# The opening of a decoder trunk: the first norm's modulation as one TensorE product in four column groups, squares on two engines, and an order written by hand

## The chip, the cores and the metric

The kernel runs on one core of a Trainium2 chip. A core has a matrix engine (TensorE, PE in the profile, with its weight loads shown apart as PEld), three engines for elementwise work (VectorE or DVE, ScalarE or ACT, GpSimd or POOL) and a queue engine (SyncE or SP) that issues most of the DMAs. The engines run side by side and wait for each other by semaphores. The metric is the device time of one execution in microseconds.

## The reference, cut to what matters

The program is a trunk of two layers over 512 tokens of width 1024, each of them an FFN half step, a mixing block and a second FFN half step. Each sub-layer begins with a norm that is modulated by the conditioning vector c:

```
c_act = silu(c)                                        # (1, 1024)
mod   = (c_act @ w_ada[l] + b_ada[l])                  # 9 rows of 1024: shift, scale, gate, ...
hn    = x * rsqrt(mean(x * x) + eps) * g * (1 + scale) + shift
h     = h + 0.5 * (1 + gate) * swiglu(hn, w_ffn1_in, w_ffn1_out)
```

Only the first norm of the first layer is touched here. It needs x, c, and the columns of `w_ada[0]` for the first shift and the first scale: 1024 by 2048 numbers in f32, 8 MB. Nothing can be multiplied before this norm has its first rows, so it is the opening of the program.

## The kernel before

Activations lie transposed: `h[0]` to `h[7]` are eight tiles of 128 channels by 512 tokens, loaded as `in_xT`. A normed activation is kept as a pair, `hnH` (rounded to the matrix engine's format fp32r) and `hnL` (the rest), and so are weights (`wH`, `wL`, made by `split` from a loaded f32 tile: a copy on ScalarE, L93, then a subtraction on VectorE, L94). `mm3` multiplies such pairs with three matmuls: wH by hnH (L88), wH by hnL (L89) and wL by hnH (L90).

`begin` (from L1064) is the opening. It loads c, an identity, the eight tiles of x and the parameters, then by `fetch(m)` the modulation's weights `wa0`, in four steps m of 2 MB, each for two tiles of channels, and between them by `fetch_w` the first four weight tiles of the FFN. All of these DMAs are issued on SP's queue in the order of the code, two for each `fetch`.

- c is spread over the 128 partitions by eight matmuls against the identity and a silu (`crep`, L1120 to L1125).
- The squares of the tiles of x are taken by ScalarE (`add_ss`, L191 and L198) and added one by one by VectorE into one tile (`ss`, L194). Four f32 matmuls against a column of ones (L1142) make sums over the channels; an f32 matmul is two instructions, so the profile has eight. ScalarE takes the square root (its table is loaded just before, L1145), VectorE the reciprocal (L1146), and four matmuls spread the result over the partitions (`ps_rstd`, L1149).
- `warm(n)` puts n matmuls on ones in front of PE, whose results nobody reads.
- `scales(m)` makes the two scale columns of step m on VectorE: each is a dot of a 128 by 1024 tile with `crep` (`ada_dot`, L151), then a small operation (L1092). `shifts(m)` makes one shift column in the same way and the other by eight f32 matmuls of one column (16 instructions, L1100).
- `normed(k)` applies the norm to tile k: times rstd on VectorE (L1105), scale and shift on ScalarE (L1107), then `split`.
- Then four output tiles of the FFN's first projection are built up over the eight channel tiles: 4 steps m, in each 8 `mm3`, which are 96 matmuls in all. In step m, after the second `mm3`, the scales, shifts and normed tiles for step m + 1 are written.

The framework's scheduler may reorder all of this on each engine by priority; the code's order is not binding. Behind the opening, `ffn` goes on with the next weight tiles through two buffers, and spends VectorE's time also on the other modulation rows (`ada_steps`, through `wadaT`, issued on GpSimd's queue); their buffers lie in memory that the opening's pool gives back.

Of the kernel before, what the change touches and what calls it, by code (L numbers as in the profile page):

```python
# [16 lines left out]
P = 128  # L17
D = 1024
T = 512
L = 2  # L20
KD = D // P
# [4 lines left out]
NB = T // P  # L26
# [31 lines left out]
def trunk_kernel(ctx, tc, ins, out, layers=L, phases=("ffn1", "mix", "ffn2")):  # L58
    nc = tc.nc
# [18 lines left out]
    def psum(shape, name, tag="x"):  # L78
        return ps.tile(shape, F32, name=name, tag=tag, bufs=2)
# [5 lines left out]
    def mm3(acc, w, k, x, sl, start, stop):  # L85

        wH, wL, xH, xL = w[0][:, k], w[1][:, k], x[0][:, sl], x[1][:, sl]
        mm(acc, wH, xH, start=start, stop=False)  # L88
        mm(acc, wH, xL, start=False, stop=False)  # L89
        mm(acc, wL, xH, start=False, stop=stop)  # L90

    def split(hi, lo, src):
        nc.scalar.copy(hi, src)  # L93
        nc.vector.tensor_sub(lo, src, hi.bitcast(F32))  # L94

    ALL = slice(0, T)
# [4 lines left out]
    cT = const.tile([P, KD], F32, name="cT")  # L101
# [3 lines left out]
    h = []  # L105
    for i in range(KD):
        t = hp_.tile([P, T], F32, name=f"h{i}")
# [5 lines left out]
    cact = const.tile([P, KD], F32, name="cact")  # L113
# [35 lines left out]
    def ada_dot(out_, w, crep):  # L149

        stt(w, w, 1.0, crep, ALU.mult, ALU.mult, accum_out=out_)  # L151
# [31 lines left out]
    def new_ss():  # L183
        return sp.tile([P, T], F32, name="ss", tag="ss")

    def add_ss(ss, i, sl=ALL):

        if ss is None:
            return
        if i == 0:  # L190
            act(ss[:, sl], h[0][:, sl], AF.Square)  # L191
        else:
            sq = square(i, sl)
            tt(ss[:, sl], ss[:, sl], sq, ALU.add)  # L194

    def square(i, sl):
        sq = E("sq")[:, sl]
        act(sq, h[i][:, sl], AF.Square)  # L198
        return sq
# [863 lines left out]
    def begin(pool):  # L1063
        hn = [tuple(hnp.tile([P, T], F32R, name=n, tag="hn") for n in ("hnH", "hnL")) for _ in range(KD)]  # L1064
        g1 = prm(0, "g1")
        bsh, bsc = (prm(0, "b_ada")[:, i * KD : (i + 1) * KD] for i in range(2))
        col = {n: pool.tile([P, KD], F32, name=n, tag=n) for n in ("sc", "sh", "gb", "gm0", "sh0")}
        stt(col["gb"], bsc, 1.0, g1, ALU.add, ALU.mult)
        wa, wf, ws = {}, [], []

        def fetch(m):
            for n in (0, 2):
                w = pool.tile([P, 2, D], F32, name="wada", tag="wada", bufs=8)
                nc.sync.dma_start(w, ins["wa0"][m, :, n : n + 2])
                wa[m, n], wa[m, n + 1] = w[:, 0], w[:, 1]
# [12 lines left out]
        def scales(m):  # L1088
            for n in range(2):
                k = slice(2 * m + n, 2 * m + n + 1)  # L1090
                ada_dot(col["sc"][:, k], wa[m, n], crep)
                stt(col["gm0"][:, k], col["sc"][:, k], g1[:, k], col["gb"][:, k], ALU.mult, ALU.add)  # L1092

        def shifts(m):
            k0, k1 = (slice(2 * m + n, 2 * m + n + 1) for n in range(2))
            ada_dot(col["sh"][:, k0], wa[m, 2], crep)
            tt(col["sh0"][:, k0], col["sh"][:, k0], bsh[:, k0], ALU.add)
            pt = psum([P, 1], "ps_ada")
            for k in range(KD):
                mm(pt, wa[m, 3][:, k * P : (k + 1) * P], cact[:, k : k + 1], start=k == 0, stop=k == KD - 1)  # L1100
            tt(col["sh0"][:, k1], pt, bsh[:, k1], ALU.add)

        def normed(k):
            z = E("z")
            tt(z, h[k], rstd, ALU.mult)  # L1105
            x = E("hn_t")
            act(x, z, AF.Identity, bias=col["sh0"][:, k : k + 1], scale=col["gm0"][:, k : k + 1])  # L1107
# [10 lines left out]
        warm(3)  # L1118

        crep = pool.tile([P, D], F32, name="crep", tag="crep")  # L1120
        for hf in range(2):
            pt = psum([P, 4, P], "ps_crep")
            for k in range(4):
                mm(pt[:, k], cT[:, 4 * hf + k : 4 * hf + k + 1].to_broadcast([P, P]), cst("ident"), start=True, stop=True)
            act(crep[:, hf * 512 : hf * 512 + 512], pt.rearrange("p k n -> p (k n)"), AF.Silu)  # L1125
        fetch(0)
        fetch_w()
        fetch_w()
        fetch(1)
        fetch_w()  # L1130
        fetch_w()
        fetch(2)
        fetch(3)
        nc.sync.dma_start(con[:, P:], ins["con"][:, P:])
        warm(20)
        ss = new_ss()
        for i in range(KD):
            add_ss(ss, i)

        pt = psum([P, NB], "ps_ss")  # L1140
        for b in range(NB):
            mm(pt[:, b : b + 1], ss[:, b * P : (b + 1) * P], ones[:, :1], start=True, stop=True)  # L1142
        warm(3)
        r = pool.tile([P, NB], F32, name="rstd_t", tag="rstd_t")
        act(r, pt, AF.Sqrt, bias=vals["eps"], scale=1.0 / D)  # L1145
        nc.vector.reciprocal(r, r)  # L1146
        rstd = psum([P, T], "ps_rstd", "r0")
        for b in range(NB):
            mm(rstd[:, b * P : (b + 1) * P], r[:, b : b + 1].to_broadcast([P, P]), cst("ident"), start=True, stop=True)  # L1149
        warm(2)  # L1150
        scales(0)
        shifts(0)
        warm(8)
        normed(0)
        split_w(0)
        split_w(1)
        normed(1)
        pts = [psum([P, T], "ps_mm", tag) for tag in ("mm", "mm", "r1", "r0")]
        for m in range(4):
            groups = [(n, 2 * m + k) for k in range(2) for n in range(4)]  # L1160
            if m == 0:
                groups = [(n, k) for n0 in (0, 2) for k in range(2) for n in (n0, n0 + 1)]
            elif m == 3:
                groups = [(n, 6 + k) for n in range(4) for k in range(2)]
            for g, (n, k) in enumerate(groups):
                mm3(pts[n], ws[n], k, hn[k], ALL, k == 0, k == KD - 1)
                if m < 3 and g == 1:
                    scales(m + 1)
                    shifts(m + 1)
                    if m == 0:  # L1170
                        split_w(2)
                        split_w(3)
                    normed(2 * m + 2)
                    normed(2 * m + 3)
# [29 lines left out]
def lay_out(i):  # L1204
    import numpy as np

    a = {}
    c = np.ascontiguousarray
# [3 lines left out]

    wT = i["w_ada"].reshape(L, D, 9, KD, P).transpose(0, 2, 3, 4, 1)
    a["wadaT"] = c(wT)
    last = i["w_ada"][0, :, :D].reshape(KD, P, 4, 2, P)[:, :, :, 1].transpose(2, 1, 0, 3).reshape(4, P, D)
    a["wa0"] = c(np.stack([wT[0, 1, ::2], wT[0, 1, 1::2], wT[0, 0, ::2], last], axis=2))
# [41 lines left out]
    r, s = np.arange(P)[:, None], np.arange(P)[None, :]  # L1258
# [26 lines left out]
```

## Time and profile before

| | us |
|---|---|
| median of 3 runs | 1956.05 (1954.79 to 1958.45) |
| span of the profiled execution | 1949.5 |
| PE busy | 1899.8 |
| VectorE busy | 1402.5 |
| ScalarE busy | 839.5 |

The profile gives the span of one execution, from its first instruction to the end of its last. The runs' times are measured apart from it, on the device, and the median lies 6.6 us above the span. In a line of the timeline stand the start, the duration, the engine, the line of the code, the operation with the tiles it writes and reads, the shapes, and a count when several are merged; in brackets stands the idle time of the engine before it and what ended it. In a line of the groups stand, behind the count, the busy time, the mean duration of one in ns, and the idle time before them. A row of the windows view has a stretch, its length, then for PE, PEld, DVE, ACT and POOL the busy time and the number of instructions, then the clock granted to PE (1.00 is full), the share of the DMA engines, and GB/s. The matmuls overlap in PE's pipeline, so the step from one start to the next tells more than the duration of one.

### The profile page before, as it was taken

To read this page: it belongs to the slowest core of one execution; us is meant where nothing else is said; L and a number is where in the kernel's file an instruction comes from. 1 tells how busy PE (TensorE), PEld (TensorE's weight loads), DVE (VectorE), ACT (ScalarE), POOL (GpSimd) and SP (SyncE) were. 2 spreads that over 40 slices of the span, in tenths; PEclk is the share of its full clock that TensorE was granted. 3 is DMA by queue.
4 is the path that set the end of the run, shared out by engine and by line. 5 is a ranking of instruction groups with operands and counts; after the bars stand their busy time and mean duration, and the time that the engine had idled before them with its cause. 6 is when DMAs were issued, how large, how long until landed. Compare 5 with 4: busy or idle time off the path is not lost.

```text
span 1949.5 us, 33127 instructions
## 1 busy us (share of the span) xinstructions
PE 1899.8 (97%) x13544; PEld 1666.5 (85%) x13544; DVE 1402.5 (72%) x2176; ACT 839.5 (43%) x1269; POOL 131.2 (7%) x212
## 2 busy tenths in 40 slices
PE   8999999999999999999999999999998999999999
PEld 6898899885677899899899989988766788998997
DVE  7687677757975787677868767776488778773862
ACT  4453255346332454155345514533553335532541
POOL 0101101100000000100100021010000000010000
PEclk8999999999999999999999999999999999999999
DMA  7667865611121475875646587662211125764732
GB/s 294 245 166 236 251 193 163 219 67 38 49 81 51 141 195 172 285 207 168 228 129 189 161 273 220 175 214 102 87 53 49 59 72 158 197 210 136 194 107 91
DMA packets 104311, 308.21 MB, mean 158 GB/s; under 512 B 23392, under 2 KB 24416, under 8 KB 103136
## 3 DMA queue, kind: packets, MB, share of 16 engines
q1 hardware_dynamic: 75936, 203.34, 30.5%
q0 software_dynamic: 28224, 102.77, 20.5%
q8 instruction: 106, 1.74, 0.4%
q14 instruction: 45, 0.37, 0.1%
HBM read 302.66 MB, written 3.41 MB: 157 GB/s over the span
## 4 chain that ended last, share of the span: by engine, by line
PE 70%; DVE 11%; DMA 10%; issue 4%; ACT 3%; POOL 1%; SPq 0%; ACTq 0%; POOLq 0%; DVEq 0%
PE ps_mm L88 11%; PE ps_mm L89 10%; PE ps_mm L90 10%; PE ps_d L369 6%; PE ps_d L371 6%; PE ps_d L370 6%; PE ps_f L369 3%; PE ps_f L371 3%; PE ps_f L370 3%; DMA wada<-in_wadaT 3%; DVE wL L94 2%; ACT wH L93 2%; PE ps_g L371 2%; PE ps_g L370 2%; PE ps_g L369 2%
## 5 line engine op out<-in xcount | busy, mean ns | idle before, releaser
L93 ACT CAST wH<-wraw 128x1024 fp32r<-128x1024 f32 (+2 forms) x292 | 269.7, 924 | 534.5 <-PE ps_mm L89 250.6
L94 DVE TENSOR_TENSOR wL<-wraw,wH 128x1024 fp32r<-128x1024 f32 (+2 forms) x292 | 309.2, 1061 | 128.7 <-ACT wH L93 127.5
L88 PE MATMUL ps_mm<-hnH,wH 128*128 128x512 f32 (+1 forms) x760 | 277.6, 371 | 9.7 <-DVE lo L552 3.4
L88 PE MATMUL ps_mm<-actH,wH 128*128 128x512 f32 (+1 forms) x744 | 282.0, 379 | 0.0
L89 PE MATMUL ps_mm<-actL,wH 128*128 128x512 f32 (+1 forms) x744 | 282.0, 379 | 0.0
L90 PE MATMUL ps_mm<-actH,wL 128*128 128x512 f32 (+1 forms) x744 | 281.7, 379 | 0.0
L89 PE MATMUL ps_mm<-hnL,wH 128*128 128x512 f32 (+1 forms) x760 | 274.8, 363 | 0.4
L90 PE MATMUL ps_mm<-hnH,wL 128*128 128x512 f32 (+1 forms) x760 | 273.4, 361 | 0.5 <-DVE wL L94 0.5
L369 PE MATMUL ps_d<-comH,wH 128*128 128x256 f32 x816 | 227.8, 279 | 3.9 <-ACT s L391 3.8
L370 PE MATMUL ps_d<-comL,wH 128*128 128x256 f32 x816 | 225.9, 277 | 0.0
L371 PE MATMUL ps_d<-comH,wL 128*128 128x256 f32 x816 | 225.6, 276 | 0.0
L151 DVE SCALAR_TENSOR_TENSOR wada<-wada,crep 128x1024 f32<-128x1024 f32 x140 | 168.0, 1221 | 53.2 <-DMA wada<-in_wadaT 53.0
L88 PEld LDWEIGHTS ps_mm<-hnH,wH 128*128 128x128 f32 x760 | 143.7, 191 | 38.0 <-issue 5.6
L94 DVE TENSOR_TENSOR wL<-sum,wH 128x1024 fp32r<-128x1024 f32 x102 | 125.0, 1225 | 68.3 <-ACT wH L93 67.9
L93 ACT CAST wH<-sum 128x1024 fp32r<-128x1024 f32 x102 | 107.5, 1054 | 150.7 <-PE ps_d L370 67.6
L89 PEld LDWEIGHTS ps_mm<-hnL,wH 128*128 128x128 f32 x760 | 145.0, 191 | 27.7 <-issue 6.4
L90 PEld LDWEIGHTS ps_mm<-hnH,wL 128*128 128x128 f32 x760 | 145.0, 191 | 22.4 <-DVE wL L94 1.1
L89 PEld LDWEIGHTS ps_mm<-actL,wH 128*128 128x128 f32 x744 | 140.7, 189 | 25.9
L90 PEld LDWEIGHTS ps_mm<-actH,wL 128*128 128x128 f32 x744 | 140.7, 189 | 25.9 <-DVE wL L94 0.3
L88 PEld LDWEIGHTS ps_mm<-actH,wH 128*128 128x128 f32 x744 | 140.5, 189 | 25.9
L369 PEld LDWEIGHTS ps_d<-comH,wH 128*128 128x128 f32 x816 | 153.5, 188 | 7.1 <-ACT s L391 5.4
L370 PEld LDWEIGHTS ps_d<-comL,wH 128*128 128x128 f32 x816 | 153.5, 188 | 0.0
(355 smaller groups left out, 3899.1 us busy)
## 6 DMA issues: line engine op xcount, KB each, us to landing
wada<-in_wadaT POOLq DMA_DIRECT2D x128, 512.0 KB, 4.9
wraw<-in_wmi SPq DMA_DIRECT2D x40, 512.0 KB
wraw<-in_w2p SPq DMA_DIRECT2D x36, 512.0 KB
wraw<-in_w1p SPq DMA_DIRECT2D x32, 512.0 KB
wraw<-in_w1o SPq DMA_DIRECT2D x32, 384.0 KB
wraw<-in_w2o SPq DMA_DIRECT2D x32, 384.0 KB
wraw<-in_w1i SPq DMA_DIRECT2D x20, 512.0 KB
wraw<-in_w1o SPq DMA_DIRECT2D x32, 320.0 KB
```

Of the source, the lines that this page charges most:

```text
L88: mm(acc, wH, xH, start=start, stop=False)
L89: mm(acc, wH, xL, start=False, stop=False)
L90: mm(acc, wL, xH, start=False, stop=stop)
L93: nc.scalar.copy(hi, src)
L94: nc.vector.tensor_sub(lo, src, hi.bitcast(F32))
L151: stt(w, w, 1.0, crep, ALU.mult, ALU.mult, accum_out=out_)
L369: mm(pt[:, i], wH, x[k][0], start=start and i + k == 0, stop=False, skip_group_check=True)
L370: mm(pt[:, i], wH, x[k][1], start=False, stop=False, skip_group_check=True)
L371: mm(pt[:, i], wL, x[k][0], start=False, stop=k == 3, skip_group_check=True)
```

## The change

The modulation of step m becomes `sums(m)` and `columns(m)`. The weights are laid out anew (`wa0`: 8 slices k of the contraction, each 128 by 512, where the 512 columns are the step's two scale and two shift tiles), and loaded by the same two DMAs of 1 MB. In `sums`, c stands still: a column of silu(c) is repeated over 32 columns of the array, and four such matmuls, for four slices k, write to the four groups of 32 output partitions; two rounds cover the eight slices. ScalarE copies the 128 by 512 result, and four f32 matmuls against a vector that picks one row of each group (`pick`) add the four groups and turn the result into four columns (`ps_col`). Three small operations of VectorE finish the scales and shifts of two tiles.

`normed` becomes three operations: VectorE scales by gain and rstd in one, ScalarE adds the shift and rounds, VectorE takes the rest. The squares are taken in turn by ScalarE (even tiles) and VectorE (odd tiles); 0 and 1 are added, 2 and 3 are added, and the six tiles that remain go to the sum matmuls one after another, with two warming matmuls behind each but the last. The table of the square root is loaded at the start by a throwaway operation (`root`). `crep` and its matmuls go; `warm(3)` and `warm(20)` at the start become `warm(8)`. From there to the end of the four steps, PE, VectorE and ScalarE must execute the instructions in the order of the code (`tc.manual_schedule`). The order of the DMAs is as before.

```diff
-        def scales(m):
-            for n in range(2):
-                k = slice(2 * m + n, 2 * m + n + 1)
-                ada_dot(col["sc"][:, k], wa[m, n], crep)
-                stt(col["gm0"][:, k], col["sc"][:, k], g1[:, k], col["gb"][:, k], ALU.mult, ALU.add)
-
-        def shifts(m):
...
+        def sums(m, between=0):
+
+            pt = psum([P, 4 * P], "ps_ada")
+            for r in range(2):
+                for c in range(4):
+                    k = 4 * r + c
+                    mm(pt[32 * c : 32 * c + 32], cact[:, k : k + 1].to_broadcast([P, 32]), wa[m, r][:, c], start=r == 0, stop=r == 1)
+                if r == 0:
+                    warm(between)
+            x = pool.tile([P, 4 * P], F32, name="asum", tag="asum", bufs=2)
+            nc.scalar.copy(x, pt)
+            return x
+
+        def columns(m, x):
+            pt = psum([P, 4], "ps_col")
+            for n in range(4):
+                mm(pt[:, n : n + 1], x[:, n * P : (n + 1) * P], pick, start=True, stop=True)
+            ks = slice(2 * m, 2 * m + 2)
+            tt(col["gm0"][:, ks], pt[:, :2], g1[:, ks], ALU.mult)
+            tt(col["gm0"][:, ks], col["gm0"][:, ks], col["gb"][:, ks], ALU.add)
+            tt(col["sh0"][:, ks], pt[:, 2:], bsh[:, ks], ALU.add)
 
         def normed(k):
-            z = E("z")
-            tt(z, h[k], rstd, ALU.mult)
-            x = E("hn_t")
-            act(x, z, AF.Identity, bias=col["sh0"][:, k : k + 1], scale=col["gm0"][:, k : k + 1])
-            split(*hn[k], x)
+            t = E("hn_t")
+            sh = col["sh0"][:, k : k + 1]
+            stt(t, h[k], col["gm0"][:, k : k + 1], rstd, ALU.mult, ALU.mult)
+            act(hn[k][0], t, AF.Identity, bias=sh)
+            stt(hn[k][1], t, sh, hn[k][0].bitcast(F32), ALU.add, ALU.subtract)
...
-        warm(20)
-        ss = new_ss()
-        for i in range(KD):
-            add_ss(ss, i)
...
+        with tc.manual_schedule(engines={mybir.EngineType.PE, mybir.EngineType.DVE, mybir.EngineType.Activation}):
+            warm(8)
+            act(root, vals["eps"], AF.Sqrt)
+            pt = psum([P, NB], "ps_ss")
+            ready = []
+            for i in range(KD):
+                sq = pool.tile([P, T], F32, name="sq", tag="sq", bufs=4)
+                if i % 2:
+                    tt(sq, h[i], h[i], ALU.mult)
+                else:
+                    act(sq, h[i], AF.Square)
+                if i in (1, 3):
+                    tt(sq, sq, before, ALU.add)
+                before = sq
+                if i in (1, 3, 4, 5, 6, 7):
+                    for b in range(NB):
+                        mm(pt[:, b : b + 1], sq[:, b * P : (b + 1) * P], ones[:, :1], start=i == 1 and b == 0, stop=i == KD - 1, skip_group_check=True)
+                    warm(2 if i < 7 else 0)
+            r = pool.tile([P, NB], F32, name="rstd_t", tag="rstd_t")
+            act(r, pt, AF.Sqrt, bias=vals["eps"], scale=1.0 / D)
+            stt(col["gb"], bsc, 1.0, g1, ALU.add, ALU.mult)
+            nc.vector.reciprocal(r, r)
+            rstd = psum([P, T], "ps_rstd", "r0")
+            for b in range(NB):
+                mm(rstd[:, b * P : (b + 1) * P], r[:, b : b + 1].to_broadcast([P, P]), cst("ident"), start=True, stop=True)
+            x = sums(0, 8)
+            warm(3)
+            columns(0, x)
+            warm(6)
+            normed(0)
+            split_w(0)
+            split_w(1)
+            normed(1)
...
+                for g, (n, k) in enumerate(groups):
+                    mm3(pts[n], ws[n], k, hn[k], ALL, k == 0, k == KD - 1)
+                    if m == 0 and g == 1:
                         split_w(2)
                         split_w(3)
+                    if m < 3 and g == 5:
+                        x = sums(m + 1)
+                    if m < 3 and g == 6:
+                        columns(m + 1, x)
+                        normed(2 * m + 2)
+                        normed(2 * m + 3)
```

More of the change, by code (lines that the diff above doesn't have):

```diff
@@ L1066, in begin @@
         bsh, bsc = (prm(0, "b_ada")[:, i * KD : (i + 1) * KD] for i in range(2))
-        col = {n: pool.tile([P, KD], F32, name=n, tag=n) for n in ("sc", "sh", "gb", "gm0", "sh0")}
-        stt(col["gb"], bsc, 1.0, g1, ALU.add, ALU.mult)
+        col = {n: pool.tile([P, KD], F32, name=n, tag=n) for n in ("gb", "gm0", "sh0")}
+        pick = pool.tile([P, 1], F32, name="pick", tag="pick")
+        nc.vector.memset(pick, 0.0)
+        for c in range(4):
+            nc.vector.memset(pick[32 * c : 32 * c + 1], 1.0)
+        root = pool.tile([P, 1], F32, name="root", tag="root")
         wa, wf, ws = {}, [], []
         def fetch(m):
[L1072 to L1075, printed above, removed]
+            for r in range(2):
+                w = pool.tile([P, 4, 4 * P], F32, name="wada", tag="wada", bufs=8)
+                nc.sync.dma_start(w, ins["wa0"][m, :, 4 * r : 4 * r + 4])
+                wa[m, r] = w
         def fetch_w():
@@ L1086, in split_w @@
             ws.append(pair)
[L1088 to L1108 removed]
+        def sums(m, between=0):
+            pt = psum([P, 4 * P], "ps_ada")
+            for r in range(2):
+                for c in range(4):
+                    k = 4 * r + c
[13 more added lines that the diff above has]
+            tt(col["sh0"][:, ks], pt[:, 2:], bsh[:, ks], ALU.add)
+        def normed(k):
+            t = E("hn_t")
[3 more added lines that the diff above has]
+            stt(hn[k][1], t, sh, hn[k][0].bitcast(F32), ALU.add, ALU.subtract)
         pw = psum([P, T], "ps_warm", "r1")
@@ L1116, in warm @@
                 mm(pw.rearrange("p (a b) -> p a b", b=P), ones_r, wide, start=True, stop=True)
[L1118 to L1125, printed above, removed]
         fetch(0)
@@ L1134, in begin @@
         nc.sync.dma_start(con[:, P:], ins["con"][:, P:])
-        warm(20)
-        ss = new_ss()
-        for i in range(KD):
-            add_ss(ss, i)
[L1140 to L1170, printed above, removed]
+        with tc.manual_schedule(engines={mybir.EngineType.PE, mybir.EngineType.DVE, mybir.EngineType.Activation}):
[31 more added lines that the diff above has]
+            normed(1)
+            pts = [psum([P, T], "ps_mm", tag) for tag in ("mm", "mm", "r1", "r0")]
+            for m in range(4):
+                groups = [(n, 2 * m + k) for k in range(2) for n in range(4)]
+                if m == 0:
+                    groups = [(n, k) for n0 in (0, 2) for k in range(2) for n in (n0, n0 + 1)]
+                elif m == 3:
+                    groups = [(n, 6 + k) for n in range(4) for k in range(2)]
+                for g, (n, k) in enumerate(groups):
+                    mm3(pts[n], ws[n], k, hn[k], ALL, k == 0, k == KD - 1)
+                    if m == 0 and g == 1:
```

6 lines of the change are left out of this document (2 added, 4 removed).

## The prediction

> **What bounds the kernel now.** I read the page's span and engine rows first, then the waits of TensorE (PE) behind the opening, then the weight loads of the first projection, counted by group, and the timeline around the last of them.
>
> ```profile
> span 1949.5 us, 33127 instructions
> PE 1899.8 (97%) x13544; PEld 1666.5 (85%) x13544; DVE 1402.5 (72%) x2176; ACT 839.5 (43%) x1269; POOL 131.2 (7%) x212
> ```
> ```profile
> PE ps_d L369 <- ACT s L391: 1.2, 1, 1.2
> ```
> ```profile
> L90 PEld LDWEIGHTS ps_mm<-hnH,wL 128*128 128x128 f32 x32 | 7.1, 222 | 1.5 <-DVE wL L94 0.2
> L88 PEld LDWEIGHTS ps_mm<-hnH,wH 128*128 128x128 f32 x32 | 7.1, 223 | 7.5 <-ACT hnH L93 3.4 <-ACT wH L93 2.8
> L89 PEld LDWEIGHTS ps_mm<-hnL,wH 128*128 128x128 f32 x32 | 7.0, 219 | 2.1 <-DVE hnL L94 0.5
> ```
> ```profile
> 21.23 0.80 PE L88 MATMUL ps_mm<-hnH,wH 128*128 128x512 f32 x1 [2.88 <-ACT hnH L93]
> ...
> 37.37 0.39 PE L90 MATMUL ps_mm<-hnH,wL 128*128 128x512 f32 x1
> 37.60 0.39 PE L88 MATMUL ps_mm<-hnH,wH 128*128 128x512 f32 x1
> ...
> 55.94 0.39 PE L90 MATMUL ps_mm<-hnH,wL 128*128 128x512 f32 x1
> 56.17 0.39 PE L88 MATMUL ps_mm<-hnH,wH 128*128 128x512 f32 x1
> ```
>
> PE is busy 97% of the span, and between 56 and 300 us the PE row shown is its only listed wait. So what the opening gains or loses reaches the end almost undiminished: later work is queued on PE, and its loads are released by that work. The opening's product is 4 steps m of 8 triples of matmuls, 96 in all; the three rows with 32 loads each, asked from 21.0 to 55.9 us, are these. The first starts at 21.23, the 97th at 56.17: that is the mark to move. At full clock one takes 0.23 us (37.37 to 37.60), 96 take 21.9, so 13 of the 35 us are modulation matmuls, waits and half clock.
>
> **The change, in the new order.** Everything below is the order as written, which PE, VectorE (DVE) and ScalarE (ACT) must now follow.
>
> *Squares and their sums.*
>
> ```profile
> 3.66 0.21 ACT L114 ACTIVATE cact<-cT 128x8 f32<-128x8 f32 x1
> 7.40 4.02 ACT L198 ACTIVATE sq<-h 128x512 f32<-128x512 f32 x6
> 12.04 0.69 DVE L194 TENSOR_TENSOR ss<-ss,sq 128x512 f32<-128x512 f32 x1
> 12.79 1.05 PE L1142 MATMUL ps_ss<-ones_r,ss 128*128 128x1 f32 x8 [0.53 <-DVE ss L194]
> 13.88 0.26 ACT L1145 ACTIVATE rstd_t<-ps_ss,v_eps 128x4 f32<-128x4 f32 x1 [1.16 <-PE ps_ss L1142]
> 14.18 0.18 DVE L1146 RECIPROCAL rstd_t<-rstd_t 128x4 f32<-128x4 f32 x1 [1.44 <-ACT rstd_t L1145]
> 15.63 1.05 PE L1149 MATMUL ps_rstd<-con,rstd_t 128*128 128x128 f32 x8
> 16.52 1.84 PE L1100 MATMUL ps_ada<-cact,wada 128*128 128x1 f32 x16
> ```
> ```profile
> L118 ACT ACT_TABLE_LOAD x1 | 1.3, 1283 | 0.8 <-PEq L1278 0.8
> ```
>
> The last of six squares started near 10.75 (7.40 + 5 x 0.67), so the last h was in by then. Today its square and add end at 12.73; with VectorE squaring it alone, at 11.5: 1.2 us gained. But four sum matmuls (8 instructions, 0.9 us of PE at the 0.11 pitch in 1.05 for eight with the drain) become six times four, with ten warming matmuls between. The first group starts near 6.9: ACT is free at 3.87, loads the square root's table 1.28, root 0.2, square 0.63, and DVE adds 0.69. h3 is in by 8.1, squared and added by 9.5. Then five groups queue: at full clock 9.5 + 5 x 0.9 + 4 x 0.46 = 15.8, against 13.84 now. At half clock it is worse:
>
> ```profile
> 1340.00 0.59 PE L217 MATMUL ps_ss<-ones_r,sq 128*128 128x1 f32 x2 [0.40 <-ACT sq L198]
> 1340.45 0.56 PE L217 MATMUL ps_ss<-ones_r,ss 128*128 128x1 f32 x2
> 1340.88 0.56 PE L217 MATMUL ps_ss<-ones_r,sq 128*128 128x1 f32 x2
> ```
> ```profile
> 12.21:15.63 3.42, 2.89 (x18) 2.51 (x18) 1.98 (x5) 0.77 (x2) 0.00 (x0) 1.00 0.99 417
> 15.63:19.04 3.41, 2.73 (x25) 2.64 (x23) 3.41 (x10) 0.13 (x1) 0.00 (x0) 1.00 1.05 425
> 19.04:22.45 3.41, 1.06 (x2) 0.56 (x2) 2.13 (x4) 3.41 (x5) 0.00 (x0) 0.50 1.00 416
> 22.45:25.87 3.42, 3.42 (x9) 2.59 (x10) 3.42 (x6) 1.99 (x3) 0.00 (x0) 0.50 1.03 414
> 25.87:29.28 3.41, 3.06 (x22) 2.48 (x20) 3.41 (x11) 0.57 (x2) 0.00 (x0) 1.00 1.02 418
> 29.28:32.69 3.41, 2.10 (x5) 1.72 (x6) 3.32 (x5) 3.12 (x5) 0.00 (x0) 0.50 1.01 421
> ```
>
> At half clock (first fence) two one-column matmuls take 0.44, eight 1.7. The second fence cuts the opening at the moments the granted clock can change, 3.41 us apart (columns: PE, PEld, DVE, ACT, POOL busy, clock, DMA). In 15.63 to 19.04 PE is 2.73 us busy, but with one-column matmuls and 0.9 us of 128-column ones: the clock falls to 0.50. In 25.87 to 29.28, 16 one-column matmuls and about five wide ones: it falls again. In 12.21 to 15.63, eight one-column and nine warming ones: it holds. So one-column matmuls don't hold the clock, and five wide ones in a stretch are too few. The new square stage offers 0.46 of warming in each 1.36 us, five wide ones a stretch, and a hole from 8.3 to 9.5 in front. I take half clock from about 9 us: 9.5 + 5 x 1.7 + 4 x 0.85 = 21.4. It returns after a stretch full of matmuls (22.45 to 25.87 did that; 29.28 to 32.69 with five did not).
>
> The Trainium skill, "TensorEngine Tiling (Array Packing)", Instruction Overhead, gives a matmul of one column some 60 cycles; by that estimate (25 ns at 2.4 GHz) six groups would cost 1.2 us and the stage would end near 11.9. Here eight took 1.05 us, so the row decides.
>
> *Up to the first main matmul.* Drain, square root 0.26, reciprocal 0.18, hand-offs (0.04 each, 14.14 to 14.18): 22.1. rstd's eight at half clock, 1.7: 23.8. The modulation weights of step 0 are no wait: their last reader of today started at 16.52.
>
> ```profile
> 446.42 1.08 PE L979 MATMUL ps_av<-pmc,V 128*64 128x512 f32 x4
> ...
> 462.56 1.02 PE L528 MATMUL ps_kk<-kksq,con 128*128 128x512 f32 x2
> ...
> 483.01 1.81 PE L730 MATMUL ps_c<-AR,a 64*64 64x128 f32 x32 [2.47 <-DVE bonus L719]
> ```
> ```profile
> L387 ACT COPY up<-ps_f 128x512 f32<-128x512 f32 x34 | 19.6, 577 | 0.0
> L235 ACT ACTIVATE hnH<-hn_t,mod 128x256 fp32r<-128x256 f32 x80 | 36.8, 504 | 33.2 <-DVE hn_t L234 33.2
> L282 DVE SCALAR_TENSOR_TENSOR h<-ps_mm,cg,h 128x512 f32<-128x512 f32 x60 | 44.9, 749 | 44.9 <-PE ps_mm L90 44.7
> L93 ACT CAST wH<-wfirst 128x1024 fp32r<-128x1024 f32 x4 | 4.2, 1039 | 1.4 <-DMA wfirst<-in_w1i 1.4
> L94 DVE TENSOR_TENSOR wL<-wfirst,wH 128x1024 fp32r<-128x1024 f32 x4 | 4.9, 1222 | 1.4 <-ACT wH L93 1.3
> L1107 ACT ACTIVATE hn_t<-z,sh,gm 128x512 f32<-128x512 f32 x8 | 6.4, 814 | 20.3 <-DVE sh L1097 20.0 <-DVE z L1105 0.2
> L93 ACT CAST hnH<-hn_t 128x512 fp32r<-128x512 f32 x8 | 4.7, 616 | 0.1
> L1101 DVE TENSOR_TENSOR sh<-ps_ada,par 128x1 f32<-128x1 f32 x4 | 0.6, 157 | 3.5 <-PE ps_ada L1100 3.5
> ```
>
> No row has four groups of 32 columns. An f32 matmul is two instructions: ps_kk's two of 512 columns take 1.02 us, some 0.43 each and the drain. Of ps_av, in two column groups of 64, four take 1.08, so they ran in pairs. ps_c put 32 on quarters of the array in 1.81, where rstd's pitch of 0.11 would make 3.6. I take four abreast: a round 0.85 us, at half clock 1.7 (bounds: in pairs, one after another). So 25.5 after the first round, about when the clock returns; eight warming 1.85, second round 0.85: 28.2. Copy with drain 0.78: 29.0. Columns 0.9 + 0.15: 30.1. Three small VectorE operations (0.16, overlapping): 30.5. Scaling by rstd 0.75 (L282's form), hnH 0.72 (between the cast's 0.62 and L1107's 0.81; L235's 0.50 is for half the columns), then wH0 1.04, which stands behind hnH in ACT's order although its weights are long there: 33.2. Today's first matmul is at 21.23: 12.0 later.
>
> *Step 0.* wL0 and wL1 (1.22 each) stand on DVE ahead of hn1: with its 0.75 + 0.72 + 0.75 and hand-offs, the third triple's second matmul starts 4.9 after wH0. Eleven matmuls 2.5, a wait for wL3 0.3, sums 1.7, triple 0.7, columns 1.0, triple 0.7: 11.8, end 45.0.
>
> *Steps 1 to 3.* In each, column matmuls, small operations, scaling and hnH make a chain of 0.15 + 0.4 + 0.75 + 0.72 + 0.1 = 2.1, covered by one triple of 0.7: PE waits 1.4 to 1.5, then 0.55 for hnL. With 24 x 0.228 = 5.5, sums 1.7, copy 0.1, columns 0.9: 10.2 for steps 1 and 2, 65.4. Step 3 has no sums but waits for hn7, 2.3 behind hn6: 9.2, to 74.6. The stretch around each tail holds about five wide matmuls, as 25.87 to 29.28 did; two of three such tails at half clock, 1.1 each: 76.8.
>
> What is taken away, 12 dots of 1.22 us on VectorE and 16 one-column instructions a step (1.84), saves PE nothing: sums and columns cost 2.6 in their place. DVE loses 14 us of work but is then not the last to finish. The crep build and its two ACT passes lay ahead of the squares' end and cost nothing today. The DMA order and bytes are unchanged. The mark moves from 56.2 to 76.8: +20.6. The span is 1949.5 and the runs' median 1956.05, 6.6 above it; I leave that part as it is: 1956.05 + 20.6 = 1976.7, given as 1977.
>
> **Rivals.** *The clock holds* if warming pairs suffice after all: stage 15.8, rstd 17.4, sums 21.0, first matmul 26.0, and no half-clock tails: 67.4, +11.2, 1967. The Trainium skill, "TensorE: Matmul & The Clock Gate", section "Why this matters for your kernels", asks only that there be no PE-idle gaps over some 3 us; the longest here is 1.2, so by it the clock holds. Against it: the 2.73 us busy and still lost. Chance 0.18.
> *The column groups don't run four abreast*, and the change does not do what its form says: in pairs 2.6 more at the start and 1.7 in each of three steps, 1984; singly three times that, about 2000. For: no row shows four streams of 128 rows. Chance 0.12.
> *The freed VectorE pays*, faster: today DVE's dots end the waits for hn_t (20.0 us in L1107's row). If the sums don't queue, step 0 is ready when its weights are, first matmul at 21.9, and PE runs at its own pace, 21.9 + 21.9 + 3 x 2.6 = 51.6: -4.6, 1951. It decides where PE's waits behind the first matmul stay under 4.6 us together; I count 11. Chance 0.05.
> *The delay is swallowed later*: no slack is seen on PE; 0.03.
>
> **How the numbers follow.** The main case has 0.62; its own bounds (hnH 0.62 to 0.81, where the clock's edges fall) give 1970 to 1983. 1965 to 1988 takes in the held clock and the pairs, and leaves out serial groups, faster and same. 0.2% (4 us) is about what a measurement of this kernel can tell from no change. Faster 0.05, same 0.03, slower 0.92.
>
> **What would show it.** Right: ps_ss in 48 instructions, half clock in most of 9 to 26 us, the first main matmul at 31 to 35, sums starting four at a time, three waits of PE for hnH of about 1.4 us, the 97th load near 77. Wrong: full clock in the square stage (then 67), or main matmuls before 22 us, or tails without a wait.

## The result, and the profile after

| | before | after |
|---|---|---|
| median of four runs, us | 1955.42 (1954.37 to 1958.45) | 1984.18 (1978.37 to 1985.07) |
| span of the profiled execution, us | 1949.5 | 1983.3 |
| first main matmul starts, us | 21.23 | 33.91 |
| 97th main matmul starts, us | 56.17 | 82.07 |

The change makes the kernel slower, by the ratio 1.0132 (interval 1.0113 to 1.0151), which on 1955 us is 25.8 us (22 to 30). The two medians lie 28.8 us apart, inside that interval; below, the ratio is used. The mark of the prediction, the start of the 97th main matmul, moved by 25.9. The page of the kernel after begins:

```profile
span 1983.3 us, 33208 instructions
...
PE 1927.9 (97%) x13599; PEld 1679.3 (85%) x13599; DVE 1390.5 (70%) x2152; ACT 833.2 (42%) x1261; POOL 130.8 (7%) x212
```

VectorE lost 12 us of work, as intended, and TensorE, which was busy 97% of the span and still is, gained 28 us. That sum also holds matmuls stretched by the halved clock, so the timeline comes next, from the squares to the first main matmul (start, duration, engine, line, operation, in brackets the idle time and its end):

```profile
7.11 1.05 PE L1154 MATMUL ps_ss<-ones_r,sq 128*128 128x1 f32 x8 [1.25 <-DVE sq L1150]
...
9.77 1.86 PE L1154 MATMUL ps_ss<-ones_r,sq 128*128 128x1 f32 x8 [1.03 <-DVE sq L1150]
11.49 1.20 PE L1127 MATMUL ps_warm<-ones_r 128*128 128x512 f32 x2
12.49 1.70 PE L1154 MATMUL ps_ss<-ones_r,sq 128*128 128x1 f32 x8
...
20.17 1.70 PE L1154 MATMUL ps_ss<-ones_r,sq 128*128 128x1 f32 x8
...
21.91 0.27 ACT L1157 ACTIVATE rstd_t<-ps_ss,v_eps 128x4 f32<-128x4 f32 x1 [9.70 <-PE ps_ss L1154]
...
24.44 1.73 PE L1098 MATMUL ps_ada<-wada,cact 128*32 128x512 f32 x8
...
28.17 1.06 PE L1098 MATMUL ps_ada<-wada,cact 128*32 128x512 f32 x8
...
29.97 1.03 PE L1108 MATMUL ps_col<-pick,asum 128*128 128x1 f32 x8
...
32.83 1.98 ACT L93 CAST wH<-wfirst 128x1024 fp32r<-128x1024 f32 x2
...
33.91 0.50 PE L88 MATMUL ps_mm<-hnH,wH 128*128 128x512 f32 x1 [1.42 <-ACT wH L93]
```

Read the gaps between the starts: from 12.49 on, one group of sums and its two warming matmuls take 2.56 us, without any idle time. VectorE's last square starts at 11.67, itself held back because TensorE had not yet freed a buffer, and ends at 12.36; the square root comes 9.55 us later. So the squares no longer bound this stage. The queue on TensorE does, and it runs at half clock, as the windows show (columns as before: PE, PEld, DVE, ACT, POOL, then the granted clock):

```profile
5.36:8.78 3.42, 2.12 (x12) 1.26 (x11) 1.94 (x3) 1.17 (x3) 0.00 (x0) 1.00 1.03 346
8.78:12.19 3.41, 2.42 (x10) 2.33 (x11) 1.99 (x4) 2.52 (x3) 0.00 (x0) 0.50 1.06 430
...
15.60:19.02 3.42, 3.42 (x16) 3.23 (x15) 0.00 (x0) 0.00 (x0) 0.00 (x0) 0.50 1.05 429
...
32.67:36.09 3.42, 1.65 (x5) 0.78 (x5) 2.95 (x3) 2.14 (x3) 0.00 (x0) 1.00 1.01 412
36.09:39.50 3.41, 2.62 (x5) 1.40 (x5) 2.44 (x4) 2.55 (x3) 0.00 (x0) 0.50 0.72 287
```

The clock is 0.50 from 8.8 to 25.8, and again from 36.1 to 42.9, 49.7 to 53.2 and 73.6 to 80.5: 34.1 us of the opening, against 13.7 before. The third row is the telling one: TensorE is busy without a gap in it and still gets half clock. What TensorE waits for up to 95 us (total, times, longest), and the end of a step:

```profile
PE ps_mm L88 <- ACT hnH L1118: 4.8, 5, 1.2
...
PE ps_mm L88 <- ACT wH L93: 1.4, 1, 1.4
PE ps_mm L89 <- DVE hnL L1119: 0.9, 3, 0.3
```
```profile
45.91 1.03 PE L1108 MATMUL ps_col<-pick,asum 128*128 128x1 f32 x8
...
47.36 0.75 DVE L1117 SCALAR_TENSOR_TENSOR hn_t<-h,gm,ps_rstd 128x512 f32<-128x512 f32 x1
48.15 0.72 ACT L1118 ACTIVATE hnH<-hn_t,sh 128x512 fp32r<-128x512 f32 x1 [2.31 <-DVE hn_t L1117]
...
48.92 0.50 PE L88 MATMUL ps_mm<-hnH,wH 128*128 128x512 f32 x1 [1.18 <-ACT hnH L1118]
...
49.71 0.79 PE L89 MATMUL ps_mm<-hnL,wH 128*128 128x512 f32 x1 [0.29 <-DVE hnL L1119]
```

That chain from columns to hnH is what the prediction described, and behind it the clock falls (49.7). In the groups of the opening, first of the kernel after and then of the kernel before, stands what TensorE itself does for the norm:

```profile
L1154 PE MATMUL ps_ss<-ones_r,sq 128*128 128x1 f32 x48 | 9.7, 324 | 2.3 <-DVE sq L1150 2.3
L1098 PE MATMUL ps_ada<-wada,cact 128*32 128x512 f32 x64 | 8.6, 644 | 0.0
L1108 PE MATMUL ps_col<-pick,asum 128*128 128x1 f32 x32 | 4.2, 251 | 0.0
```
```profile
L1100 PE MATMUL ps_ada<-cact,wada 128*128 128x1 f32 x64 | 7.4, 245 | 0.0
L1142 PE MATMUL ps_ss<-ones_r,ss 128*128 128x1 f32 x8 | 1.1, 253 | 0.5 <-DVE ss L194 0.5
```

### The profile page after: what moved, and what is told of

Its sections match the earlier page's. It is cut to its first block, busy times and chain, and to the rows that moved or that the text cites. A ratio compares the mean times of both kernels' runs of the same rounds, so it can differ in the third digit from the quotient of the medians.

```text
span 1983.3 us, 33208 instructions
## 1 busy us (share of the span) xinstructions
PE 1927.9 (97%) x13599; PEld 1679.3 (85%) x13599; DVE 1390.5 (70%) x2152; ACT 833.2 (42%) x1261; POOL 130.8 (7%) x212
## 3 DMA queue, kind: packets, MB, share of 16 engines
q0 software_dynamic: 28224, 102.77, 20.7%
HBM read 302.66 MB, written 3.41 MB: 154 GB/s over the span
## 4 chain that ended last, share of the span: by engine, by line
PE 76%; DVE 9%; DMA 8%; issue 3%; ACT 2%; SPq 0%; POOL 0%; ACTq 0%; DVEq 0%; POOLq 0%
PE ps_mm L88 13%; PE ps_mm L89 12%; PE ps_mm L90 12%; PE ps_d L369 6%; PE ps_d L371 6%; PE ps_d L370 6%; PE ps_f L369 3%; PE ps_f L371 3%; PE ps_f L370 3%; DMA wada<-in_wadaT 2%; DVE wL L94 2%; PE ps_g L371 2%; PE ps_g L370 2%; PE ps_g L369 2%; ACT wH L93 1%
## 5 line engine op out<-in xcount | busy, mean ns | idle before, releaser
L88 PE MATMUL ps_mm<-hnH,wH 128*128 128x512 f32 (+1 forms) x760 | 282.0, 376 | 11.1 <-ACT hnH L1118 4.8
L151 DVE SCALAR_TENSOR_TENSOR wada<-wada,crep 128x1024 f32<-128x1024 f32 x128 | 153.5, 1221 | 51.3 <-DMA wada<-in_wadaT 51.2
L88 PEld LDWEIGHTS ps_mm<-hnH,wH 128*128 128x128 f32 x760 | 145.2, 193 | 43.6 <-issue 8.3
L89 PEld LDWEIGHTS ps_mm<-actL,wH 128*128 128x128 f32 x744 | 140.8, 189 | 25.8
L88 PEld LDWEIGHTS ps_mm<-actH,wH 128*128 128x128 f32 x744 | 140.8, 189 | 25.8
```

## The experiments

The theory at the start was the prediction's: TensorE is queued behind six groups of sums at half clock, and the tails of the steps leave it idle. Its rivals were that the halved clock alone is the loss, that the order written by hand is, and that the operations themselves cost too much. All times of marks below are from the traces; "mark" is the first weight load of the 97th main matmul, which the trace has at 55.94 before and at 81.84 after.

**Squares as before** (all else as in the change).

```diff
-            warm(8)
+            warm(32)
             act(root, vals["eps"], AF.Sqrt)
...
-                if i % 2:
-                    tt(sq, h[i], h[i], ALU.mult)
-                else:
-                    act(sq, h[i], AF.Square)
...
-                if i in (1, 3, 4, 5, 6, 7):
-                    for b in range(NB):
...
-                    warm(2 if i < 7 else 0)
+            ss = new_ss()
+            for i in range(KD):
+                add_ss(ss, i)
+            pt = psum([P, NB], "ps_ss")
+            for b in range(NB):
+                mm(pt[:, b : b + 1], ss[:, b * P : (b + 1) * P], ones[:, :1], start=True, stop=True)
+            warm(2)
```

> The squares and their sum as before (ScalarE squares, VectorE adds, one group of sum matmuls), 32 warming matmuls ahead of it; all else as in the change. Theory: six queued groups of one-column matmuls at half clock cost the start. Then rstd is ready near 15.5 instead of 24.4, the clock is full until the first round of the modulation, the first main matmul starts near 23.5 (33.9 in the change) and the 97th load near 71 (81.8), so about 1973 us. Rival, that the order by hand behind the squares is the cost and the weights' arrival sets the start: first matmul not before 30, time within 4 us of the change.

Measured: first main matmul at 23.58 and mark at 70.19, as the theory expected (23.5 and 71), ratio to before 1.0074 (1.0046 to 1.0101). Its opening:

```profile
12.10 1.05 PE L1146 MATMUL ps_ss<-ones_r,ss 128*128 128x1 f32 x8 [0.61 <-DVE ss L194]
...
14.81 1.06 PE L1098 MATMUL ps_ada<-wada,cact 128*32 128x512 f32 x8
...
17.84 1.06 PE L1098 MATMUL ps_ada<-wada,cact 128*32 128x512 f32 x8
...
23.58 0.50 PE L88 MATMUL ps_mm<-hnH,wH 128*128 128x512 f32 x1 [1.43 <-ACT wH L93]
```

The square root starts at 13.19 instead of 21.91, and the clock stays full until 26.2. So the new square stage costs 10.3 us at the first matmul and 11.7 at the mark, somewhat less than half of the loss.

**No warming between the sums, and seven instead of two.** The first kernel, then the second:

```diff
-                    warm(2 if i < 7 else 0)
+                    warm(0)
```
```diff
-                    warm(2 if i < 7 else 0)
+                    warm(7 if i < 7 else 0)
```

> No warming matmuls between the six groups. Theory: the ten warming matmuls do not hold the clock, they only stand in the queue at half speed, 0.85 us a pair: the square stage ends 3.5 to 4.3 us earlier (21.9 to about 18), the first main matmul near 30, the 97th load near 78. Rival, that they hold up the clock: the stage ends no earlier, and the half-clock stretch grows longer than from 8.8 to 25.8.

> Seven warming matmuls between the six groups instead of two. Theory: 1.6 us of warming in each 2.5 us holds the clock at 1.00 through the square stage, but the warming stands in the same queue: five groups of 0.9 and four times 1.6 end near 20.7, only about 1 us before the 21.9 of the change at half clock; first main matmul near 31. Rival, that half clock alone is what the stage loses: it ends near 16.

Measured without warming: the square root starts at 19.46, the mark is 79.62, the ratio 1.0102 (1.0068 to 1.0135). The square root is only 2.45 earlier than in the change, but the second group also began later, since tiles 2 and 3 of x came later in this execution:

```profile
10.73 8.69 PE L1154 MATMUL ps_ss<-ones_r,sq 128*128 128x1 f32 x40 [2.56 <-DVE sq L1150]
```

Counted from the second group's start to the square root, it is 8.73 us (five groups at 1.70 and the hand-off) against 12.14 in the change (9.77 to 21.91): 3.4 less, just under the 3.5 to 4.3 expected. With seven:

```profile
11.47 3.33 PE L1127 MATMUL ps_warm<-ones_r 128*128 128x512 f32 x7
14.60 1.38 PE L1154 MATMUL ps_ss<-ones_r,sq 128*128 128x1 f32 x8
15.84 1.87 PE L1127 MATMUL ps_warm<-ones_r 128*128 128x512 f32 x7
17.55 0.95 PE L1154 MATMUL ps_ss<-ones_r,sq 128*128 128x1 f32 x8
```

From 15.5 on the clock is full again, and a group takes 0.95 instead of 1.70. Yet from the second group (9.91) to the square root (23.55) are 13.64 us, 1.5 more than with two: the warming matmuls take more time than the clock gives back. The mark is 81.74, and the one run took 1982.62. So the rival that the halved clock alone makes the loss falls, and the expectation of 20.7 with it; two warming matmuls don't hold the clock and only lengthen the queue; seven bring it back, but after two stretches at half clock (8.7 to 15.5) and at too high a price.

**Weights split ahead of the first modulation**, so that wL0 and wL1 don't stand before hn1 on VectorE nor wH0 behind hnH on ScalarE.

```diff
+            split_w(0)
+            split_w(1)
             x = sums(0, 8)
...
             normed(0)
-            split_w(0)
-            split_w(1)
             normed(1)
```

> The first two weight tiles are split ahead of the first modulation sums, not behind the first normed tile. Theory: the order put 1.0 us of ScalarE ahead of the first matmul and 2.4 us of VectorE ahead of the second normed tile: first main matmul near 32.9 (33.9), the third triple near 35.2 (37.7), step 0 without half clock, 97th load 3 to 5 us earlier (77 to 79). Rival, that PE's own work and the later tails set the pace: less than 1.5 us.

Measured: mark 75.02, 6.8 earlier where 3 to 5 was expected; ratio 1.0099 (1.0066 to 1.0131). The first row of its main matmuls:

```profile
32.03 0.50 PE L88 MATMUL ps_mm<-hnH,wH 128*128 128x512 f32 x1 [0.51 <-ACT hnH L1118]
```

The wait that was 1.42 for wH is 0.51 for hnH. From there to step 1 are 11.7 us instead of 15.0, and the clock stays full from 25.9 to 66.8: without the holes of step 0, the half-clock stretch of 36.1 to 42.9 is gone too. Of the 6.8, 1.7 came earlier: its square root starts at 20.20, though that stage is the change's own. Its second group of sums began at 8.46 instead of 9.77, because tiles 2 and 3 of x were there sooner in this execution. So about 5 us are this edit's, at the upper end of what was expected. They lie in step 0 and behind it: the first main matmul itself starts 11.8 us after the square root, where it was 12.0, and not the 1.0 sooner that was expected. The clock comes back at 25.9 in both traces, so the first sums with their eight warming matmuls, which began earlier here, ran longer at half clock (4.5 us from 22.73 to 27.22, against 3.7 from 24.44 to 28.17).

**Sums and columns earlier in the step**, so that four triples of matmuls (three in step 0) instead of one stand between columns and the next step.

```diff
-                    if m < 3 and g == 5:
+                    if m < 3 and g == (2 if m else 3):
                         x = sums(m + 1)
-                    if m < 3 and g == 6:
+                    if m < 3 and g == (3 if m else 4):
                         columns(m + 1, x)
```

> The next step's sums stand behind the third triple (fourth in step 0) and its columns one triple later, so that four triples (three in step 0) cover the chain to the next normed tile. Theory: three waits of 1.2 us for hnH and 0.3 for hnL go, and with them the half clock of 49.7 to 53.2 and 73.6 to 80.5: 97th load 6 to 9 us earlier (73 to 76). Rival, that the matmuls of sums and columns on PE are the cost of the steps, not the chain: under 3 us.

Measured: mark 69.63, 12.2 earlier where 6 to 9 was expected; ratio 1.0067 (1.0047 to 1.0087). Its waits up to 83 us, with the three tails gone:

```profile
PE ps_mm L88 <- ACT hnH L1118: 1.4, 2, 0.8
PE ps_mm L88 <- ACT wH L93: 1.4, 1, 1.4
PE ps_mm L90 <- DVE wL L94: 0.7, 2, 0.5
```

Of the 12.2, 2.7 came ahead of the first main matmul (31.17), in the unchanged square stage (second group at 8.28, and half clock only from 9.9). The other 9.5 are just above the range: 27 matmuls of the change stand 0.43 behind the one before them, the pace at half clock, and only 3 here, the others 0.23, which is 4.8; the rest is in shorter waits, those for hnH 1.4 instead of 4.8. What half clock is left (33.9 to 40.7) falls mainly on the sums of step 0, which take 3.04 instead of 1.85. In the change an idle tail costs its own length and, behind two of the three, the halved clock of the stretch that follows.

**The same operations in the scheduler's order**: the line with `tc.manual_schedule` is taken out and its block stands free.

> The change without the order by hand: PE, VectorE and ScalarE are ordered by the framework's scheduler, as before. Theory: the six groups of one-column matmuls stay in PE's queue and the scheduler moves the weight splits ahead and spreads the sums; 97th load between 66 and 76 (81.8), 5 to 12 us faster than the change and still slower than before. Rival, that the loss lies in the operations and not in their order: within 4 us of the change.

Measured: first main matmul 29.51, mark 69.33, ratio 1.0078 (1.0056 to 1.0099). The order written by hand costs 12.5 us at the mark, where 5 to 12 was expected: 4.4 of them ahead of the first main matmul and 8.1 behind it. In the scheduler's order the operations, squares included, keep the other 13.4 of the loss.

**All of it mended**: squares as before, sums and columns early, round 1 of the first sums ahead of the spread of rstd, weights' roundings on ScalarE ahead of the first norm, and the weights' rests on VectorE in the pause in which it waits for hnH.

`split_h` makes wH, `split_l` wL; the spread and three warming matmuls stand between the two rounds of the first sums.

```diff
-            x = sums(0, 8)
+            x = sums(0, spread_rstd)
             warm(3)
             columns(0, x)
-            warm(6)
-            normed(0)
-            split_w(0)
-            split_w(1)
-            normed(1)
+            warm(8)
+            split_h(0)
+            split_h(1)
+            normed(0, 0)
+            normed(1, 1)
...
         def normed(k, middle=None):
...
             act(hn[k][0], t, AF.Identity, bias=sh)
+            if middle is not None:
+                split_l(middle)
             stt(hn[k][1], t, sh, hn[k][0].bitcast(F32), ALU.add, ALU.subtract)
```

> All of the costs taken out together, with the TensorE modulation and an order by hand kept: squares as before with 32 warming matmuls; the first round of sums in front of the spread of rstd, the second behind it; the first two weight tiles rounded on ScalarE ahead of the first normed tile; sums and columns of the next step behind the third and fourth triple. Theory: first main matmul near 21 us, steps near PE's own 5.5 + 2.6 us, 97th load at 51 to 54 (55.9 before), so 2 to 5 us faster than the kernel before. Rival, that the two extra TensorE products a step cost more than VectorE's dots did, whatever the order: 97th load at 57 or later, not faster than before.

Measured: first main matmul 21.39, mark 56.45 where 51 to 54 was expected; 1952.87 against 1953.13 of the kernel before, ratio 1.0001 (0.9983 to 1.0018). So the loss is repaired wholly and nothing is gained. The mark lies between the theory's 54 and the rival's 57, and "not faster" is what the rival said. Since this kernel keeps the new sums and columns and loses nothing, the loss isn't in these operations as such, but in what stands around them: their place, that of the weights, and the squares. Its opening and one step:

```profile
14.80 1.16 PE L1164 MATMUL ps_rstd<-con,rstd_t 128*128 128x128 f32 x8
...
21.39 0.51 PE L88 MATMUL ps_mm<-hnH,wH 128*128 128x512 f32 x1
22.43 0.50 PE L89 MATMUL ps_mm<-hnL,wH 128*128 128x512 f32 x1 [0.53 <-DVE hnL L1121]
...
25.92 0.40 PE L90 MATMUL ps_mm<-hnH,wL 128*128 128x512 f32 x1
26.24 1.92 PE L1098 MATMUL ps_ada<-wada,cact 128*32 128x512 f32 x16
28.10 0.50 PE L88 MATMUL ps_mm<-hnH,wH 128*128 128x512 f32 x1
...
28.67 0.40 PE L90 MATMUL ps_mm<-hnH,wL 128*128 128x512 f32 x1
28.90 1.03 PE L1108 MATMUL ps_col<-pick,asum 128*128 128x1 f32 x8
29.79 0.48 PE L88 MATMUL ps_mm<-hnH,wH 128*128 128x512 f32 x1
```

From 25.92 to 28.10 are 2.18 us where a plain step is 0.23, so the sums cost TensorE 1.95; in the same way columns cost 0.89. The kernel before has this in the same place:

```profile
26.28 0.39 PE L90 MATMUL ps_mm<-hnH,wL 128*128 128x512 f32 x1
26.52 1.84 PE L1100 MATMUL ps_ada<-cact,wada 128*128 128x1 f32 x16
28.22 0.48 PE L88 MATMUL ps_mm<-hnH,wH 128*128 128x512 f32 x1
```

That is 1.71. The new modulation thus costs TensorE 2.84 a step for 1.71, in three steps 3.4 us more, and the 12 dots of 1.22 us that it takes from VectorE don't come back as time: in this kernel the opening has no half clock (before, 13.7 us) and some 3.5 us of waits, and still ends where the old one does. That a still tighter order would gain was not tried.

**Both kernels a second time**, unchanged, for a second trace.

> The kernel before, unchanged, for a second trace. The traces of the change and its variants lose 2 to 8 us more behind the opening than in it, at stretches of half clock near 400, 460, 505 and 1010 us that the first trace of before lacks. Theory: where the 3.41 us stretches fall differs from run to run, and the first trace of before was a lucky one; a second one shows other stretches and a span some us longer. Rival, that the change costs time later in the program: the second trace is like the first.

> The kernel with the change, profiled a second time, to see what of the 7.9 us that it lost behind the 97th load (1901.5 us from there to the end of the span, against 1893.5 and 1895.5 in the two traces of the kernel before) is its own. The theory, that this is where the free 3.41 us stretches of the clock fall, expects a remainder anywhere between 1895 and 1902, with half clock at other places behind 90 us, and the opening unchanged within what those stretches move (97th load at 79 to 83). The rival, that the change leaves something behind that slows the later work, expects a remainder of 1901 to 1902 again, with half clock at the same places.

Measured: before, mark 55.52, span 1951.0, time 1953.32; after, mark 81.27, span 1984.1, time 1985.9. From the mark to the end of the span it is 1893.5 and 1895.5 in the two traces of before, 1901.5 and 1902.8 in those of after, and 1895.1 to 1902.4 in the other kernels. The second trace of after fits neither expectation cleanly. Its remainder is the rival's. Of its half-clock stretches behind the mark most stand within 4 us of those of the first trace (near 407, 470, 510, 1020 and 1472), but those at 1370 and 1517 have no counterpart there, nor have the first trace's at 575 and 1688 one here.

What makes the remainder long can be read off the granted clock. Behind the mark the traces of before have 15.5 and 18.8 us of half clock, those of after 32.2 and 34.0. At half clock half of the time is lost; with that half taken off, the remainders are 1885.8 and 1886.1 before and 1885.4 and 1885.8 after (1883.2 to 1886.2 in the other kernels, but 1889.5 in the scheduler's order). So between before and after the half-clock stretches are the whole difference, and the later work is otherwise not slower. Nor are their places the change's own: less the 25.9 by which the mark moved, 407, 510, 1018 and 1472 are 381, 484, 992 and 1446, and the traces of before have half clock at 382, 483, 993 and 1444, each in one of the two. Whether the change makes more of these places fall is a question for the timed runs. The column on the right is the ratio less one, times 1955 us:

| kernel | mark later than before, us | time later than before, us (interval) |
|---|---|---|
| the change | 25.9 | 25.8 (22.1 to 29.5) |
| no warming between sums | 23.7 | 19.9 (13.3 to 26.4) |
| weights split first | 19.1 | 19.4 (12.9 to 25.6) |
| squares as before | 14.3 | 14.5 (9.0 to 19.7) |
| sums and columns earlier | 13.7 | 13.1 (9.2 to 17.0) |
| scheduler's order | 13.4 | 15.2 (10.9 to 19.4) |
| all mended | 0.5 | 0.2 (-3.3 to 3.5) |

In each kernel the time moved by what the mark moved, within the interval. So the loss lies in the opening, and the 7 to 8 us that single traces show behind it are not seen in the timed runs. Why more stretches fell to half clock in both profiled executions of the change than in those of before stays open.

## Why the prediction was right, and where its sum was short

Slower was forecast, 1977 us, and 1984.18 was measured. That is inside the stated range of 1965 to 1988, but above the 1970 to 1983 that the prediction gave for its own main case: the range reached so far up for column groups that run in pairs, whose time, 1984, was put almost exactly where the measurement fell. They don't run in pairs, as shown below, so that the time still fell in the range is in part luck. The mechanism was right and one term was too small.

**The bound.** Right: what the opening loses reaches the end undiminished, in seven kernels.

**The square stage.** Right in kind and size. Half clock was taken from about 9 to a stretch full of matmuls; it was 8.8 to 25.8. The end of the sums was put at 21.4 and the square root began at 21.91.

**Up to the first main matmul.** Right: 33.2 was given, 33.91 measured, with the stages between 0.3 and 1.1 late. The four column groups ran abreast: eight instructions in 1.06 at full clock and 1.73 at half, drain included, where 0.85 and 1.7 without it had been taken. ScalarE's order put wH0 behind hnH, and the first matmul waited 1.42 for it. (The early load of the square root's table did not serve: the silu of c came behind it, and the table was loaded again at 10.93, beside other work.) So the rival of groups in pairs falls, though the time alone would have fitted it.

**The rival of the held clock** failed, and the row that the prediction set against it (2.73 of 3.41 us busy and the clock lost) was the right one to trust. The Trainium skill, "TensorE: Matmul & The Clock Gate", section "Why this matters for your kernels", asks for no idle gaps of TensorE over some 3 us; here the longest gap between TensorE's first matmul and the fall was 1.25, and the clock stayed at half in windows without any. The measurement decides. In the prediction's aside on one-column matmuls of 25 ns, a stage with 1.2 us for six groups would end near 12.3, not 11.9; the stage ended at 21.9, far from both.

**The freed VectorE** was a bound that no order here reached: 51.6 needed steps of 2.6 of modulation without waits. They cost 2.84, and about 3.5 us of waits stayed even in the mended kernel.

**Steps 0 to 3: here the sum was short.** From the first to the 97th main matmul it gave 43.6 us; the trace has 48.2, which with the 0.7 of the start makes 25.9 out of 20.6. Counted by the starts of the matmuls:

| term | predicted, us | measured, us |
|---|---|---|
| matmuls behind half clock | 2.2 | 6.4 (27 steps of 0.43 for 0.23, three of 0.59) |
| sums and the hand-off of their copy, three times | 5.4 | 5.8 |
| columns, three times | 2.8 | 2.8 |
| tail waits for hnH and hnL, three times | 6.0 | 5.7 |
| waits of step 0 and for hn7 | 5.3 | 4.2 |
| 96 matmuls at full pace, with what refilling the pipeline adds | 21.9 | 23.2 |

The failed term is the first, "two of three such tails at half clock, 1.1 each". The stretch that the prediction had quoted, with about five wide matmuls in it, gave the rule rightly; but step 0, with its waits for hn1 and for wL, was not put to it. Its two stretches in the windows above, 32.67 to 36.09 and 36.09 to 39.50, have five main matmuls each in their rows (one stands in both): from 36.09 on 6.8 us of half clock follow, which were charged at nothing. The wait for hn1 and the pace behind it:

```profile
37.72 0.79 PE L88 MATMUL ps_mm<-hnH,wH 128*128 128x512 f32 x1 [0.61 <-ACT hnH L1118]
...
39.52 0.63 PE L88 MATMUL ps_mm<-hnH,wH 128*128 128x512 f32 x1
39.95 0.63 PE L89 MATMUL ps_mm<-hnL,wH 128*128 128x512 f32 x1
```

Two of three tails at half clock was right in number, but in step 3 the clock fell for two stretches, not one; the wait for hn7 (0.68, up to 73.92) reaches into the second. In all, five stretches of the steps ran at half clock where the sum had two.

**The 6.6 us outside the span** were not there. The second runs have the time 2.3 and 1.8 us above their own spans; the rest of the 6.6 was that the first profiled execution was quicker than the median run. Leaving the difference as it was did no harm, since it cancels.

**Why the order by hand lost**, which the prediction had only as a count of waits, is shown by two edits. From the first main matmul to the mark the change takes 47.9 us, with the sums moved two or three triples ahead 38.5, in the scheduler's order 39.8: in the steps the move recovers all that the scheduler's order does. The scheduler's other 4.4 us lie ahead of the first main matmul, and no run takes them apart. The prediction took the order as written; that most of the loss in the steps was in the place of sums and columns was not said there.

## What to carry to other kernels

Moving work onto the engine that bounds the kernel has to be paid in that engine's time first: a tile sent to the sum matmuls cost TensorE 0.9 us, where adding it on VectorE, beside TensorE, cost 0.69. When an order is written by hand, count the covered time between an operation's last input and its first reader, and charge an idle tail for its length and, where too few wide matmuls are left in its stretch of 3.4 us, for the halved clock that follows. And judge what holds the clock by rows of the kernel in which it fell, not by how busy the engine looks.

## What the runs showed of the hardware

Eight f32 matmul instructions of one column, with their loads of 128 columns, take 0.9 us at full clock and 1.56 to 1.7 at half, and they do not keep the clock up: a window with 16 instructions on TensorE, busy in all of its 3.42 us, stayed at 0.50, while seven matmuls of 512 columns between the groups brought it back after two stretches. Busy time alone doesn't tell: in the change, 59.97 to 63.39 had TensorE busy for 2.01 us, in matmuls of 512 columns, and the clock held; in the kernel before, 15.63 to 19.04 had it busy for 2.73, largely in one-column matmuls, and the clock fell.

The moments at which the clock can change lie 3.41 us apart, and their phase differs from one execution to the next: the half-clock stretch that begins at 36.09 in one trace of the change begins at 35.5 in the other. The Trainium skill, "TensorE: Matmul & The Clock Gate", section "What's actually happening", says that the window runs freely and doesn't start with the kernel; the traces agree.

The change's square stage is also more sensitive to when the first tiles of x land than one group of sums at the end is, behind which the square root starts between 13.19 and 14.31 in four traces (both of before, squares as before, all mended). In four traces that have the change's square stage the second group starts at 8.28, 8.46, 9.47 and 9.77, and the square root, in the same order, at 18.84, 20.20, 21.45 and 21.91. With the clock's phase that makes 3 us, so a difference of 2 or 3 us in one trace of this stage is not yet the edit's.
